# A decoder layer in one kernel: load order of a weight pair, sums of squares folded ahead of TensorE, one of the last multiplications moved to GpSimd

## The chip, the cores and the metric

The kernel runs on one core of one Trainium2 chip. The time is the device time of one execution in microseconds (us), and the median of the runs stands for a kernel. One execution is taken with the hardware profiler; its trace gives the start and length of every instruction. The engines are called PE (TensorE), DVE (VectorE), ACT (ScalarE), POOL (GpSimd) and SP (SyncE, which issues the DMA transfers here).

## The reference

`x` is 1024 tokens by 1024 features, `mem` 256 tokens by 1024, all in float32, one layer:

```python
h = rmsnorm(x, ln1); z = h @ w_in                      # x and mem: sums of squares over the features
x = x + concat(mlstm(z), forgetting_attention(z)) @ w_out
x = x + cross_attention(rmsnorm(x, ln_x), rmsnorm(mem, ln_mem), w_xq, w_xkv, w_xo)
u = relu(rmsnorm(x, ln2) @ w_ff1)                      # up projection, 1024 -> 4096
x = x + (u * u) @ w_ff2                                # down projection
return rmsnorm(x, ln_f)
```

`rmsnorm(x, g)` is `x * rsqrt(mean(x*x) + eps) * g` for each token. The mLSTM part has gates of each token (log-sigmoid, cumulative sums) and a short causal convolution ahead of it.

## The kernel before

Features lie on the 128 partitions and tokens along the free axis. Every float32 product is done as three matmuls in a reduced format: `split` cuts an operand into a high part (ACT, L134) and the rest (DVE, L135), and `mm3` issues the matmuls of lines L186 to L188. Weight tiles of 128x1024 are loaded to `wr` or `z` and cut into `wh` and `wl`.

**Order.** A scheduler with a simulated timeline decides, when the program is built, in which order the instructions of each engine stand, except inside `in_order()` blocks, which keep the written order (the start of the kernel, and the last part). On the chip each engine works through its queue strictly in that order. PSUM banks go by names (`mm`, `tp`, `m2`, `sc`, `ov`), and a new tile of a name waits until an old one of it has been read out.

**Stages.** First come the values and gates of the mLSTM, with the sums of squares of `x` (two halves of 512 tokens) and of `mem`; then projections, the heads of the mLSTM, forgetting attention, cross attention, the up projection, the down projection, and the last part with the final norm.

**Sums of squares.** ACT squares pairs of feature tiles into the 128x1024 tiles `wide`, and DVE adds these up (`add_to`, L370), so that the two feature tiles of a pair stand side by side: element `[p, e*512 + t]`. `rsqrt_sums` sums over the partitions with matmuls against a column of ones (L234). It needs two matmuls for each 128 tokens, one for each `e`. For one half of `x` that is 8 matmuls, for `mem` 4, and `rsqrt_cols` makes the inverse roots `rcol` of them on DVE and POOL.

**Gates.** The gate values get their log-sigmoid by a polynomial on DVE (L440), then PE transposes them (`mm`, `sc`: L456; `tp`, `sc`: L461), and DVE runs two scans (L462, L466) along the tokens.

**Up projection.** Each pair of weight tiles `r1`, `r2` (128x1024, four blocks x11, x12, x21, x22 of 512) feeds seven products instead of eight. `raw_pair` (L1235) loads both tiles, `left_up` cuts blocks and has POOL form the sums of blocks: first `x21 + x22`, both in `r2` (L1256), then three differences (L1223) and a last addition (L1260). The products of the pairs follow one another with weights prepared five products ahead. POOL also folds parts of the results (L1223, `r_f`).

**The end.** The tokens of the last half are done in two quarters of 256. `finish` sums the squares (L1603), makes the inverse roots, spreads them over the partitions into a PSUM bank (`spread`, L213), and DVE multiplies four tiles of 128x2x256 by them (L1617), each followed by its store on SP's queue (L1618).

Of the kernel before, what the change touches and what calls it, by code (L numbers as in the profile page):

```python
# [11 lines left out]
AF = mybir.ActivationFunctionType  # L12
ALU = mybir.AluOpType
# [4 lines left out]
P = 128  # L18
T = 1024
TH = 512  # L20
D = 1024
KT = D // P
NM = 256
# [21 lines left out]
def hybrid_layer(ctx: ExitStack, tc: tile.TileContext, a: dict, out: bass.AP):  # L45
    nc = tc.nc
    v, s, g = nc.vector, nc.scalar, nc.gpsimd
# [31 lines left out]
    def w2(tag, n=512, dt=F32, p=P):  # L79
        return sb("r_" + tag, [P, 512], BUFS[tag], dt)[:p, :n]  # L80
# [15 lines left out]
    def ov_():  # L96
        return ps_tile("ov")
# [16 lines left out]
    ones = const("ones", [P, 1])  # L114
# [79 lines left out]
    def rsqrt_cols(out_, sums, scale, n, over=None):  # L194

        var = col("var", n)
        if over is None:
            v.tensor_scalar(out=var, in0=sums, scalar1=scale, scalar2=EPS, op0=ALU.mult, op1=ALU.add)
        else:
            e = col("t", n)  # L200
            v.scalar_tensor_tensor(out=e, in0=over, scalar=EPS, in1=over, op0=ALU.mult, op1=ALU.mult)
            v.scalar_tensor_tensor(out=var, in0=sums, scalar=scale, in1=e, op0=ALU.mult, op1=ALU.add)
        y = col("y", n)
        g.tensor_tensor(out=y, in0=var, in1=half[:, :n], op=ALU.pow)
        t = col("t", n)
        v.tensor_tensor(out=t, in0=y, in1=y, op=ALU.mult)
        v.scalar_tensor_tensor(out=t, in0=t, scalar=-0.5, in1=var, op0=ALU.mult, op1=ALU.mult)
        v.scalar_tensor_tensor(out=out_, in0=t, scalar=1.5, in1=y, op0=ALU.add, op1=ALU.mult)

    def spread(ps, cols, n):  # L210

        for t in range(n):
            nc.tensor.matmul(ps[:, t * P : (t + 1) * P], cols[:, t : t + 1].broadcast_to([P, P]), ident, start=True, stop=True)  # L213

    def sum_cols(ps, src, n):
        for t in range(n):
            nc.tensor.matmul(ps[:, t : t + 1], src[:, t * P : (t + 1) * P], ones, start=True, stop=True)

    def square_sum(acc, x, first, by=s, add=v):
        sq = acc if first else w2("c")[:, : x.shape[-1]]  # L220
        if by is s:
            s.activation(sq, x, AF.Square)
        else:
            by.tensor_tensor(out=sq, in0=x, in1=x, op=ALU.mult)
        if not first:
            add.tensor_tensor(out=acc, in0=sq, in1=acc, op=ALU.add)

    def rsqrt_sums(acc, r, nt, parts=1, bank=None, over=None):

        ps = (bank or ov_)()  # L230
        for t in range(nt):
            for e in range(parts):
                at = (e * nt + t) * P
                nc.tensor.matmul(ps[:, t : t + 1], acc[:, at : at + P], ones, start=e == 0, stop=e == parts - 1)  # L234
        rsqrt_cols(r, ps[:, :nt], 1.0 / D, nt, over)

    def rsqrt_row(acc, r, nt, parts=1, bank=None, over=None):

        rsqrt_sums(acc, r, nt, parts, bank, over)
        rb = (bank or ov_)()  # L240
        spread(rb, r, nt)
        return rb[:, : nt * P]

    rowd = dram.tile([4, T], F32, name="rowd")

# [10 lines left out]
    rcol = const("rcol", [P, 8])  # L256
# [11 lines left out]
    at = 0  # L268
# [10 lines left out]
    rcol_m = const("rcol_m", [P, 2])  # L279

    def mem_prepare():
        acc = w2("b")
        for i in range(KT // 2):
            raw = w2("ffde"[i])
            load(raw.rearrange("p (k c) -> p k c", k=2), a["mem"][:, 2 * i : 2 * i + 2])
            traced = len(nc.cur_bb.bb.instructions)
            square_sum(acc, raw, i == 0)
            hi = w2("p", dt=F32R)
            for e in range(2):
                c = slice(e * NM, e * NM + NM)  # L290
                gain = vec[:, VEC["ln_mem"] + 2 * i + e :][:, 0:1]
                split(hi[:, c], raw[:, c].bitcast(F32R), raw[:, c], gain)
            for x in nc.cur_bb.bb.instructions[traced:]:
                if i > 1 and x.engine == mybir.EngineType.Activation:
                    tc.add_manual_dep(
                        x,
                        last_evicted.name,
                        mybir.DependencyInfo(mybir.DependencyClass.NoSync, mybir.DependencyReason.DATA),
                        reason="behind the first values",
                    )  # L300
            for p_, t in enumerate((hi.bitcast(F32), raw)):
                load(hmd[:, p_, 2 * i : 2 * i + 2], t.rearrange("p (k c) -> p k c", k=2))
        rsqrt_sums(acc, rcol_m, 2, 2)


    xa = act(F32)
# [21 lines left out]
    raws = [sb("wr", [P, 1024], 2) for _ in range(2)]  # L328
    wg_raw = z4()[:, : KT * 16].rearrange("p (k c) -> p k c", k=KT)
    for k in range(KT):  # L330
        if k == 1:
            load(wg_raw, a["w_gate"])
        if k % 2 == 0:
            c = slice(k % 4 * 256, k % 4 * 256 + 512)
# [28 lines left out]
    wide = [w4() for _ in range(3)]  # L363
# [5 lines left out]
    def add_to(t, u):  # L369
        return v.tensor_tensor(out=t, in0=t, in1=u, op=ALU.add)  # L370
# [3 lines left out]
    z, e, q, lf = (small[:, i:j].rearrange("p (t c) -> p t c", c=c) for i, j, c in ((0, 128, GC), (128, 224, GW), (224, 320, GW), (320, 416, GW)))  # L374
# [6 lines left out]
    with in_order():  # L381
        for k in range(KT):
            cut_w(k)
            cut_x(0, k)
            if k in (0, 2, 4):
                cut_gates(k // 2)
            if k in (1, 3, 5):
                square_to(wide[k // 2], 0, k)
            if k == 4:
                add_to(wide[0], wide[1])  # L390
            first_values(0, k, range(4))
        square_to(wide[1], 0, 7)
        cut_x(1, 0)
        add_to(wide[0], wide[2])
        cut_x(1, 1)
        add_to(wide[0], wide[1])
        for k in range(2, 6):
            cut_x(1, k)
        for k in range(KT):
            if k in (2, 3):  # L400
                cut_x(1, k + 4)
            if k == 2:
                square_to(wide[1], 1, 1)
            if k == 4:
                square_to(wide[2], 1, 3)
            first_values(1, k, range(3))
            if k == 1:
                rsqrt_sums(wide[0], rcol[:, 0:4], 4, 2)
            if 2 < k < 7:
                first_sink(0, k - 3)  # L410
            if k == 6:
                add_to(wide[1], wide[2])
                square_to(wide[0], 1, 5)
        square_to(wide[2], 1, 7)
        add_to(wide[1], wide[0])
        last_sum = add_to(wide[1], wide[2])
    tiles[1].append(ps_tile("mm")[:, :WV])
    for k in range(KT):
        first_values(1, k, (3,))
    rsqrt_sums(wide[1], rcol[:, 4:8], 4, 2)  # L420
    for t in range(4):
        first_sink(1, t)
    last_evicted = next(i for i in reversed(nc.cur_bb.bb.instructions) if i.engine == mybir.EngineType.Activation)
# [5 lines left out]
    ps = ov_()  # L429
# [263 lines left out]
    for _ in range(2):  # L693
        t = act().rearrange("p a b -> p (a b)").rearrange("p (i c) -> p i c", i=4)
# [404 lines left out]
    n = 0  # L1099
# [36 lines left out]
    for n0 in (0, 4):  # L1136
        ws = [weights(a["w_out_b"][n0 // 2 + i], 6 * P) for i in range(2)]
        for hf in range(2):
            if len(h2) <= hf:
                h2.append((act(), act()))  # L1140
            for n in range(n0, n0 + 4):
                w = both(ws[n // 2 % 2], lambda t: t.rearrange("p (k c) -> p k c", k=3)[:, :, n % 2 * P : n % 2 * P + P])
                ps = mm()
# [87 lines left out]

    def raw_pair(p_, n0, n1):
        raws = [sb("wr", [P, 1024], 2) if p_ % 2 else z4()[:, :1024] for _ in range(2)]
        for raw, n in zip(raws, (n0, n1)):
            load(raw, a["w_ff1"][n])  # L1235
        return raws

    todo = [(b, k, 4 * b + k, 4 * b + 2 + k) for b in range(NB) for k in range(2)]

# [354 lines left out]
    def finish(acc, hf, c0, wid, parts):  # L1594

        n = wid // P
        r, var, e, y_, t = (col(c, n) for c in ("r", "var", "den", "y", "t"))
        over = inv[:, 4 * hf + c0 // P :][:, :n]
        v.scalar_tensor_tensor(out=e, in0=over, scalar=EPS, in1=over, op0=ALU.mult, op1=ALU.mult)
        ps = bank()  # L1600
        for i in range(n):
            for k in range(parts):
                nc.tensor.matmul(ps[:, i : i + 1], acc[:, k * wid + i * P :][:, :P], ones, start=k == 0, stop=k == parts - 1)  # L1603
        v.scalar_tensor_tensor(out=var, in0=ps[:, :n], scalar=1.0 / D, in1=e, op0=ALU.mult, op1=ALU.add)
        g.tensor_tensor(out=y_, in0=var, in1=half[:, :n], op=ALU.pow)
        yield
        v.tensor_tensor(out=t, in0=y_, in1=y_, op=ALU.mult)
        v.scalar_tensor_tensor(out=t, in0=t, scalar=-0.5, in1=var, op0=ALU.mult, op1=ALU.mult)
        v.scalar_tensor_tensor(out=r, in0=t, scalar=1.5, in1=y_, op0=ALU.add, op1=ALU.mult)
        yield  # L1610
        rb = bank()[:, :wid]
        spread(rb, r, n)
        rb = rb.rearrange("p (o c) -> p o c", o=1).broadcast_to([P, 2, wid])
        yield
        for k in range(0, KT, 2):
            y = x2[k // 4][:, k // 2 % 2, :, hf, c0 : c0 + wid]
            v.tensor_tensor(out=y, in0=y, in1=rb, op=ALU.mult)  # L1617
            load(out[:, k : k + 2, hf * TH + c0 : hf * TH + c0 + wid], y)  # L1618
            yield

# [82 lines left out]
```

## Time and profile before

| | before |
|---|---|
| median of 3 runs | 1522.53 us (1522.43 to 1523.9) |
| the profiled execution | 1523.35 us |
| its span in the trace | 1521.6 us |
| granted TensorE clock | 0.998 |
| busy: PE / DVE / ACT / POOL | 1502.7 / 1100.3 / 727.7 / 510.1 us |
| matmuls on PE | 7694 |

The span runs from the first to the last instruction that the trace shows; 1.75 us of the profiled execution lie around it. Times in the trace count from the span's start. A row of the timeline has the start, the length, the engine, the line, the operation, what is written and read, and, in brackets, how long the engine sat idle ahead of it and what ended that. A PE row's length overlaps the next; consecutive 128x512 matmuls start 0.23 us apart.

### The profile page before, as it was taken

Reading aid. Unit: us, or ns where it says so; the run is one execution under the profiler, and the core shown is the slowest. Engines: PE = TensorE matmul, PEld = TensorE weight load, DVE = VectorE, ACT = ScalarE, POOL = GpSimd, SP = SyncE. Lnnn points to the kernel's source line nnn. Section 1 sums busy time; section 2 is a strip of 40 time slices with the busy share of each in tenths; the row PEclk is TensorE's granted clock in tenths of the full one; section 3 lists DMA queues with packets and bytes.
Section 4 is the critical chain, followed back from the end, with each engine's and each line's share of the span. In section 5 each row is a group of like instructions: output and inputs, shape, how many; then the busy total and the mean of one; then the engine's idle time right before and its main releaser. Section 6 shows DMA issues by size and latency. Waiting matters only on the chain.

```text
span 1521.6 us, 21977 instructions
## 1 busy us (share of the span) xinstructions
PE 1502.7 (99%) x7694; PEld 1261.5 (83%) x7694; DVE 1100.3 (72%) x1743; ACT 727.7 (48%) x1360; POOL 510.1 (34%) x543
## 2 busy tenths in 40 slices
PE   9999999999999999999999999999999999999997
PEld 9988888889999788888888877778787888888887
DVE  7766676765787786944457989898887667787665
ACT  7324343334687665644443456666664621122124
POOL 1003030413364442511110034544555265663322
PEclk9999999999999999999999999999999999999999
DMA  6322223435888886843344437776678777776623
GB/s 239 109 77 87 98 100 114 135 126 157 246 244 267 260 264 230 300 131 124 119 147 157 153 134 277 247 256 242 222 252 286 291 277 276 276 270 248 239 94 111
DMA packets 122538, 299.86 MB, mean 197 GB/s; under 512 B 13614, under 2 KB 28264, under 8 KB 115516
## 3 DMA queue, kind: packets, MB, share of 16 engines
q1 hardware_dynamic: 122428, 298.46, 57.4%
q8 instruction: 60, 0.98, 0.3%
q14 instruction: 50, 0.41, 0.1%
HBM read 199.60 MB, written 98.81 MB: 196 GB/s over the span
## 4 chain that ended last, share of the span: by engine, by line
PE 93%; DVE 3%; ACT 2%; DMA 1%; issue 1%; SPq 0%; DVEq 0%; POOLq 0%; POOL 0%; ACTq 0%
PE tp L186 8%; PE tp L187 8%; PE tp L188 8%; PE m L186 6%; PE sc L186 6%; PE m L187 6%; PE m L188 6%; PE sc L187 6%; PE sc L188 6%; PE mm L186 6%; PE mm L187 6%; PE mm L188 6%; PE ov L186 2%; PE ov L187 2%; PE ov L188 2%; PE ov L801 2%
## 5 line engine op out<-in xcount | busy, mean ns | idle before, releaser
L186 PE MATMUL tp<-act,wl 128*128 128x512 f32 (+1 forms) x440 | 172.9, 393 | 1.2 <-ACT row L1396 0.7
L187 PE MATMUL tp<-act,wh 128*128 128x512 f32 (+1 forms) x440 | 172.1, 391 | 0.0
L188 PE MATMUL tp<-act,wh 128*128 128x512 f32 (+1 forms) x440 | 171.7, 391 | 0.0
L135 DVE TENSOR_TENSOR wl<-wr,wh 128x1024 fp32r<-128x1024 f32 (+2 forms) x95 | 124.5, 1311 | 22.0 <-ACT wh L134 21.4
L134 ACT ACTIVATE wh<-wr 128x1024 fp32r<-128x1024 f32 (+2 forms) x95 | 95.6, 1007 | 75.9 <-PE tp L188 34.7
L186 PE MATMUL mm<-act,wl 128*128 128x512 f32 (+1 forms) x332 | 127.5, 384 | 0.0
L188 PE MATMUL mm<-act,wh 128*128 128x512 f32 (+1 forms) x332 | 127.3, 383 | 0.0
L187 PE MATMUL mm<-act,wh 128*128 128x512 f32 (+1 forms) x332 | 127.2, 383 | 0.0
L186 PE MATMUL m<-act,wl 128*128 128x512 f32 (+1 forms) x308 | 117.7, 382 | 0.5 <-DVE wl L135 0.5
L188 PE MATMUL m<-act,wh 128*128 128x512 f32 (+1 forms) x308 | 117.7, 382 | 0.0
L187 PE MATMUL m<-act,wh 128*128 128x512 f32 (+1 forms) x308 | 117.5, 381 | 0.0
L186 PEld LDWEIGHTS tp<-act,wl 128*128 128x128 f32 x440 | 82.6, 188 | 20.6 <-ACT row L1396 1.2
L188 PEld LDWEIGHTS tp<-act,wh 128*128 128x128 f32 x440 | 82.6, 188 | 18.9
L187 PEld LDWEIGHTS tp<-act,wh 128*128 128x128 f32 x440 | 82.7, 188 | 18.5
L186 PE MATMUL sc<-act,wl 128*128 128x512 f32 (+1 forms) x248 | 97.0, 391 | 1.0 <-DVE wl L135 1.0
L188 PE MATMUL sc<-act,wh 128*128 128x512 f32 (+1 forms) x248 | 96.7, 390 | 0.0
L187 PE MATMUL sc<-act,wh 128*128 128x512 f32 (+1 forms) x248 | 96.6, 390 | 0.0
L1467 POOL TENSOR_TENSOR z<-wr 128x256 f32<-128x256 f32 x56 | 51.7, 944 | 130.6 <-DMA wr<-w_ff2q 116.8
L134 ACT ACTIVATE wh<-z 128x1024 fp32r<-128x1024 f32 (+1 forms) x54 | 55.5, 1028 | 80.8 <-POOL z L1467 58.4
L135 DVE TENSOR_TENSOR wl<-z,wh 128x1024 fp32r<-128x1024 f32 (+1 forms) x54 | 74.3, 1376 | 7.8 <-ACT wh L134 7.6
L134 ACT ACTIVATE w<-wr 128x768 fp32r<-128x768 f32 (+2 forms) x31 | 25.5, 823 | 106.2 <-PE tp L186 33.7
L188 PEld LDWEIGHTS mm<-act,wh 128*128 128x128 f32 x332 | 62.3, 188 | 12.7
(726 smaller groups left out, 4288.4 us busy)
## 6 DMA issues: line engine op xcount, KB each, us to landing
act<-right SPq DMA_DIRECT2D x49, 1024.0 KB
right<-w SPq DMA_DIRECT2D x56, 256.0 KB
wr<-w_ff2q SPq DMA_DIRECT2D x28, 512.0 KB
right<-r_d SPq DMA_DIRECT2D x49, 256.0 KB
right<-r_e SPq DMA_DIRECT2D x49, 256.0 KB
act<-fqk SPq DMA_DIRECT2D x48, 256.0 KB
wr<-w_in SPq DMA_DIRECT2D x20, 512.0 KB
wr<-w_ff SPq DMA_DIRECT2D x20, 512.0 KB
```

What stands on the lines that cost most here:

```text
L134: s.activation(hi, src, AF.Copy)
L135: return v.tensor_tensor(out=lo, in0=src, in1=hi.bitcast(F32), op=ALU.subtract)
L186: nc.tensor.matmul(ps, w[1], x[0], start=first, stop=False, skip_group_check=more)
L187: nc.tensor.matmul(ps, w[0], x[1], start=False, stop=False, skip_group_check=more)
L188: nc.tensor.matmul(ps, w[0], x[0], start=False, stop=last, skip_group_check=more)
L801: nc.tensor.matmul(self.ov[:, c0:], self.fv[:, self.j], t[:, c0:], start=self.j == 0 and t is self.p[1], stop=self.last and t is self.p[0])
L1467: g.tensor_tensor(out=o, in0=x, in1=y, op=op)
```

## The change

There are three edits, and the scheduler's answer to them.

1. `raw_pair` issues the load of the second tile of a pair, `r2`, ahead of that of `r1`. The places of the loads in SP's queue stay.
2. A new helper `fold` adds the second half of a tile of sums to its first half on DVE. It stands behind the last `add_to` of each half of `x` (128x512) and behind the squares of `mem` (128x256). The sums over the partitions then take half the matmuls, through `sum_cols` (L217): 4, 4 and 2 in place of 8, 8 and 4.
3. In `finish`, for the last quarter alone, the second multiplication is done otherwise: ACT copies the spread roots from PSUM to `r_c` (L1615), and POOL multiplies the 128x2x256 tile by them (L1616). Its store stays the second of the last four in the program's text.

```diff
+    def fold(x, n):
+        return v.tensor_tensor(out=x[:, :n], in0=x[:, :n], in1=x[:, n : 2 * n], op=ALU.add)
...
-    def rsqrt_sums(acc, r, nt, parts=1, bank=None, over=None):
-        ps = (bank or ov_)()
-        for t in range(nt):
-            for e in range(parts):
-                at = (e * nt + t) * P
-                nc.tensor.matmul(ps[:, t : t + 1], acc[:, at : at + P], ones, start=e == 0, stop=e == parts - 1)
-        rsqrt_cols(r, ps[:, :nt], 1.0 / D, nt, over)
+    def rsqrt_sums(acc, r, nt):
+        ps = ov_()
+        sum_cols(ps, acc, nt)
+        rsqrt_cols(r, ps[:, :nt], 1.0 / D, nt)
...
-        rsqrt_sums(acc, rcol_m, 2, 2)
+        fold(acc, NM)
+        rsqrt_sums(acc, rcol_m, 2)
...
         add_to(wide[0], wide[1])
+        fold(wide[0], TH)
...
-                rsqrt_sums(wide[0], rcol[:, 0:4], 4, 2)
+                rsqrt_sums(wide[0], rcol[:, 0:4], 4)
...
-        last_sum = add_to(wide[1], wide[2])
+        add_to(wide[1], wide[2])
+        last_sum = fold(wide[1], TH)
...
-    rsqrt_sums(wide[1], rcol[:, 4:8], 4, 2)
+    rsqrt_sums(wide[1], rcol[:, 4:8], 4)
...
-        for raw, n in zip(raws, (n0, n1)):
+        for raw, n in zip(raws, (n1, n0)):
             load(raw, a["w_ff1"][n])
-        return raws
+        return raws[::-1]
...
+            if k == 2 and hf and c0:
+                rs = w2("c", wid)
+                s.activation(rs, rb, AF.Copy)
+                g.tensor_tensor(out=y, in0=y, in1=wide_(rs), op=ALU.mult)
+            else:
+                v.tensor_tensor(out=y, in0=y, in1=wide_(rb), op=ALU.mult)
```

Since the scheduler is run again, the queues change beyond the edited lines: PE's order in the start (behind the first values) and around the end of cross attention, with that of DVE and ACT there, and POOL's in the up projection. The helpers' lines move by 3 to 7, so L456, L461 and L477 of before are L452, L457 and L473 now, L1396 is L1392, L1372 is L1368, L1256 is L1252, and L1223 is L1219.

PE, behind the projections that follow the first values. `tp` in the first row and `sc`, `mm` are projections of 128x256; L456 and L461 are the transposes of the gates; the `tp` and `m` with 128x512 use the next two weight tiles. Before:

```order
L188 MATMUL tp_678<-wh_505,act_104 128x256
L456 MATMUL mm_622<-ident,w_29_148 12x128 x4
L456 MATMUL sc_628<-ident,w_29_148 12x128 x4
L461 MATMUL sc_634<-ident,w_29_148 4x128 x4
L186 MATMUL sc_705<-wh_499,act_105 128x256
...
L477 MATMUL ov_759<-ident,act_486 128x4 x8
L186 MATMUL tp_887<-act_104,wl_856 128x512
...
L186 MATMUL m_95_928<-act_102,wl_925 128x512
```

The same place in the changed kernel:

```order
L188 MATMUL tp_672<-wh_499,act_105 128x256
...
L186 MATMUL tp_880<-act_104,wl_849 128x512
...
L452 MATMUL mm_616<-ident,w_29_148 12x128 x4
L452 MATMUL sc_622<-ident,w_29_148 12x128 x4
L457 MATMUL sc_628<-ident,w_29_148 4x128 x4
L186 MATMUL sc_699<-wh_493,act_105 128x256
...
L473 MATMUL ov_753<-ident,act_480 128x4 x8
L186 MATMUL m_95_921<-act_102,wl_918 128x512
```

The 24 matmuls of the 128x512 `tp` stood between the transposes' followers (L477) and `m`; now they stand ahead of the transposes, right behind the `tp` of 128x256, and `m` follows L473 directly. On DVE the split that makes the weights of `m` stands behind both scans, before and now; of the changed kernel:

```order
L458 SCALAR_TENSOR_TENSOR act_480<-w_41_481,act_480 12x1024
L461 TENSOR_TENSOR act_480<-sc_628,act_480 4x512
L461 TENSOR_TENSOR act_480<-tp_633,act_480 4x512
L138 SCALAR_TENSOR_TENSOR w_64_774<-act_480,w_63_773 12x1024
L462 SCALAR_TENSOR_TENSOR act_480<-act_480 4x1024
L138 SCALAR_TENSOR_TENSOR act_107<-sc_699,rcol,act_107 128x2x128
L135 TENSOR_TENSOR wl_918<-wr_915,wh_917 128x1024
```

Here L458 and L462 are the two scans; they wait for the transposes, and `wl_918` is what `m_95_921` reads. Nothing in this row of seven moved against another.

PE around the end of cross attention, where `tp` and `sc` are the banks of one output tile each, filled in two passes (`act_8402`, then `act_8601`), and the second pass of a bank waits until ACT has read the first. Before:

```order
L188 MATMUL sc_9143<-act_8402,wh_9063 128x512
L186 MATMUL tp_9125<-act_8601,wl_8790 128x512
...
L186 MATMUL m_1717_9202<-act_8728,wl_9118 128x512
...
L186 MATMUL ov_9246<-act_8729,wl_9118 128x512
...
L186 MATMUL sc_9143<-act_8601,wl_9064 128x512
```

The same place in the changed kernel:

```order
L188 MATMUL mm_9069<-act_7775,wh_9048 128x512
L186 MATMUL tp_9118<-act_8594,wl_8783 128x512
...
L186 MATMUL sc_9136<-act_8395,wl_9057 128x512
...
L188 MATMUL tp_9118<-act_8594,wh_8782 128x512
...
L186 MATMUL sc_9136<-act_8594,wl_9057 128x512
...
L186 MATMUL m_1717_9195<-act_8721,wl_9111 128x512
```

Before, 12 matmuls of `m` and 9 of `ov` stood between the second pass of `tp` and that of `sc`; now the second pass of `sc` follows the last four matmuls of `tp` directly, and `m` comes behind it. The second pass of `tp`, in turn, now has 24 matmuls of `mm` between itself and the first. ACT's queue holds, now as before, the cut of a weight tile, the read of `tp` and the read of `sc` in this order there.

POOL in the up projection, one window of it; L1256 (now L1252) is `x21 + x22` of a pair, and `r_f` is a fold of a result. Before:

```order
L1260 TENSOR_TENSOR wr_9435<-wr_9435,r_c_9444 128x512
L1223 TENSOR_TENSOR r_f_9515<-w_1749_9470,r_f_9515 128x512
L1256 TENSOR_TENSOR wr_9776<-wr_9776 128x512
L1223 TENSOR_TENSOR z_1767_9606<-z_1767_9606,z_1766_9605 128x512
```

The same window in the changed kernel:

```order
L1256 TENSOR_TENSOR wr_9429<-wr_9429,r_c_9437 128x512
L1252 TENSOR_TENSOR wr_9768<-wr_9768 128x512
L1219 TENSOR_TENSOR r_f_9508<-w_1749_9463,r_f_9508 128x512
L1219 TENSOR_TENSOR z_1766_9598<-z_1766_9598,z_1767_9599 128x512
```

The addition now stands ahead of the fold `r_f` in two of every three windows; in the third it stays behind it. In all of them it waits for the first load of its pair, where it waited for the second.

At the end, DVE's four multiplications of the last quarter become three, and ACT and POOL get one instruction each; SP's last four stores stand in another order, the second and third of them exchanged.

More of the change, by code (lines that the diff above doesn't have):

```diff
@@ L226, in square_sum @@
             add.tensor_tensor(out=acc, in0=sq, in1=acc, op=ALU.add)
-    def rsqrt_sums(acc, r, nt, parts=1, bank=None, over=None):
-        ps = (bank or ov_)()
-        for t in range(nt):
-            for e in range(parts):
-                at = (e * nt + t) * P
-                nc.tensor.matmul(ps[:, t : t + 1], acc[:, at : at + P], ones, start=e == 0, stop=e == parts - 1)
-        rsqrt_cols(r, ps[:, :nt], 1.0 / D, nt, over)
[L237 to L242, printed above, removed]
+    def rsqrt_sums(acc, r, nt):
+        ps = ov_()
+        sum_cols(ps, acc, nt)
+        rsqrt_cols(r, ps[:, :nt], 1.0 / D, nt)
     rowd = dram.tile([4, T], F32, name="rowd")
@@ L1612, in finish @@
         spread(rb, r, n)
-        rb = rb.rearrange("p (o c) -> p o c", o=1).broadcast_to([P, 2, wid])
+        wide_ = lambda x: x.rearrange("p (o c) -> p o c", o=1).broadcast_to([P, 2, wid])
         yield
@@ L1616, in finish @@
             y = x2[k // 4][:, k // 2 % 2, :, hf, c0 : c0 + wid]
-            v.tensor_tensor(out=y, in0=y, in1=rb, op=ALU.mult)
+            if k == 2 and hf and c0:
[4 more added lines that the diff above has]
+                v.tensor_tensor(out=y, in0=y, in1=wide_(rb), op=ALU.mult)
             load(out[:, k : k + 2, hf * TH + c0 : hf * TH + c0 + wid], y)
```

## The prediction

> **What bounds the kernel now.** I read the page first, then PE's waits, then the chain of waits in the three regions that the change touches, and the timelines of the engines there.
>
> ```profile
> span 1521.6 us, 21977 instructions
> ...
> PE 1502.7 (99%) x7694; PEld 1261.5 (83%) x7694; DVE 1100.3 (72%) x1743; ACT 727.7 (48%) x1360; POOL 510.1 (34%) x543
> ```
>
> PE is busy for 1502.7 of 1521.6 us. So a microsecond is gained only where PE has fewer matmuls to issue, where one of its few waits goes, or behind its last matmul; one is lost wherever a new wait opens in PE's queue. PE's waits name what there is to win:
>
> ```profile
> PE mm L213 <- DVE c_r L1609: 1.6, 1, 1.6
> ...
> PE sc L186 <- DVE wl L135: 1.0, 2, 0.5
> ...
> PE tp L186 <- DVE wl L135: 0.5, 1, 0.5
> PE m L186 <- DVE wl L135: 0.5, 1, 0.5
> ```
>
> The columns are total, times and longest. Four waits of 0.5 us for a weight split (`wl`) lie in the up projection. The wait for `c_r` belongs to the final norm and stays.
>
> **Part one, the folds.** The chain shows what the sums cost on PE:
>
> ```profile
> 23.08 1.68 PE ov L234 x16
> ...
> 39.71 1.68 PE ov L234 x16
> ...
> 74.40 0.79 PE ov L234 x8
> ```
>
> Each written matmul shows as two records. Half of them go: 0.84 + 0.84 + 0.39 = 2.07 us less on PE. DVE gets three additions for it. The same operation at the fold's size, and the last addition ahead of the first fold, are these:
>
> ```profile
> 20.86 1.22 DVE L370 TENSOR_TENSOR w<-w,w 128x1024 f32<-128x1024 f32 x1
> ...
> 45.96 0.68 DVE L226 TENSOR_TENSOR r_b<-r_c,r_b 128x512 f32<-128x512 f32 x1
> ```
>
> The addition ends at 22.08, the fold at about 22.7, and PE comes to the sums at 23.08: 0.3 us to spare, so the first fold is hidden, as the cuts behind it on DVE are needed later still. The other two stand where PE has other matmuls queued ahead of the sums. I take the folds at nothing and the gain at **-2.07**. If the 0.3 us were gone, the price is at most the fold's 0.68.
>
> **What the scheduler moved in the start.** The 24 matmuls of 128x512 `tp` now follow the 128x256 `tp` directly, and the gates' transposes come behind them. Two waits follow. PE's rows of before, from the chain (first the transposes' end and the moved group, then `m`) and the timeline:
>
> ```profile
> 54.28 0.60 PE L456 MATMUL mm<-ident,w 128*12 128x128 f32 x4
> ```
>
> ```profile
> 61.41 0.58 PE ov L477 x8
> 61.99 0.43 PE tp L186
> ...
> 67.78 0.24 PE m L186
> ```
>
> What ACT and DVE do for them:
>
> ```profile
> 54.43 0.47 ACT L137 ACTIVATE act<-tp,rcol 128x256 fp32r<-128x256 f32 x1 [2.35 <-PE tp L188]
> ```
>
> ```profile
> 54.94 0.48 DVE L138 SCALAR_TENSOR_TENSOR act<-tp,rcol,act 128x256 fp32r<-128x256 f32 x1 [0.71 <-ACT act L137]
> 56.02 2.28 DVE L462 TENSOR_TENSOR_SCAN act<-w,act 12x1024 f32<-12x1024 f32 x1 [0.60 <-ACT act L457]
> ...
> 60.74 2.27 DVE L466 TENSOR_TENSOR_SCAN act<-act 4x1024 f32<-4x1024 f32 x1
> ...
> 63.31 1.20 DVE L135 TENSOR_TENSOR wl<-wr,wh 128x1024 fp32r<-128x1024 f32 x1
> ```
>
> First wait: the moved group takes the bank of the 128x256 `tp`, so it starts only when ACT and DVE have read that. Before, PE was free at 54.28 and the second read ended at 55.42 (54.94 + 0.48): about **+1.2** with the signal. Second wait: the weights of `m` are cut behind two scans, and the scans need the transposes. From the first transpose to the end of the cut: 63.31 + 1.20 - 54.28 = 10.2 us. Between transpose and `m` PE had work until 67.78, which covered it by 3.3 us; without the moved group's 5.8 us (61.99 to 67.78) the work ends 7.7 us after the transpose, and PE waits 10.2 - 7.7 = 2.5, with the restart **+2.6**. Both are waits that the trace of before doesn't show. From below their bound is nothing (if the scheduler's picture holds on the chip), from above 1.2 and 2.6; I take the upper end, since the chain is made of rows of this same place.
>
> **The end of cross attention.** ACT and PE of before:
>
> ```profile
> 876.27 0.50 PE L186 MATMUL tp<-act,wl 128*128 128x512 f32 x1 [0.73 <-ACT row L1396]
> ...
> 879.18 0.39 PE L186 MATMUL m<-act,wl 128*128 128x512 f32 x1
> ...
> 884.08 0.39 PE L186 MATMUL sc<-act,wl 128*128 128x512 f32 x1
> ```
>
> ```profile
> 879.38 1.06 ACT L134 ACTIVATE wh<-wr 128x1024 fp32r<-128x1024 f32 x1 [2.11 <-PE tp L188]
> 880.34 0.58 ACT L1372 ACTIVATE r_p<-tp 128x512 f32<-128x512 f32 x1
> 880.82 0.59 ACT L1396 ACTIVATE row<-sc 128x512 f32<-128x512 f32 x1
> ```
>
> The wait at 876.27 (0.73 idle; 0.9 with the restart, as 0.50 idle makes 0.66 in the up projection below) goes, because 24 other matmuls now stand in between. But `sc`, which came at 884.08, now follows the second pass of `tp`, whose end was 879.18. It needs the read that ended at 881.41, behind a cut and a read that themselves wait for that pass. That makes a wait of 881.41 - 879.18 = 2.2, with the restart 2.35; net **+1.45**. Its lower bound is -0.9, if ACT gets to the read earlier.
>
> **Part two, the load order.** DVE, POOL and PE in one of the four windows with a wait for `wl`, and DVE at the same work in the next window:
>
> ```profile
> 1015.44 0.69 DVE L1383 TENSOR_TENSOR r_p<-sc,r_p 128x512 f32<-128x512 f32 x1 [1.18 <-PE sc L188]
> ...
> 1017.85 2.39 DVE L135 TENSOR_TENSOR w<-w,r_e 128x512 fp32r<-128x512 f32 x2
> ...
> 1036.12 1.29 DVE L135 TENSOR_TENSOR w<-w,r_d 128x512 fp32r<-128x512 f32 x2
> ```
>
> ```profile
> 1018.37 1.31 POOL L1256 TENSOR_TENSOR wr<-wr 128x512 f32<-128x512 f32 x1 [5.79 <-DMA wr<-w_ff]
> 1019.65 1.75 POOL L1223 TENSOR_TENSOR z<-z,z 128x512 f32<-128x512 f32 x1
> ```
>
> ```profile
> 1023.64 0.40 PE L188 MATMUL tp<-act,wh 128*128 128x512 f32 x1
> 1024.54 0.50 PE L186 MATMUL m<-act,wl 128*128 128x512 f32 x1 [0.50 <-DVE wl L135]
> ```
>
> ```profile
> 1009.21 0.33 SPq L1235 DMA_DIRECT2D wr<-w_ff  x1
> ...
> 1013.69 0.33 SPq L1235 DMA_DIRECT2D wr<-w_ff  x1
> ```
>
> POOL had waited 5.79 us for the second load of a pair, which took 4.68 us from its issue (1013.69 to 1018.37); when it came, the addition ran beside DVE's splits, and two of those took 2.39 us instead of 1.29: DVE lost 1.1 us, and PE's next start came 0.90 after the last, 0.66 more than the usual 0.24. With `r2` loaded first, the addition's data is there as long after 1009.21, at 1013.9, and it runs where DVE has 1.18 us idle (to 1015.44). DVE's 1.1 us come back, more than the 0.66 that PE waits. Four such windows: **-2.65**. The bound on the other side is nothing, if the waits stay. What could be late next is the cut of `r1`, now loaded second: but the pair loaded here is `wr`, while the window still works on the pair in `z`, so the cut has the rest of the window; I take nothing for it.
>
> [...]
>
> **Part three, the end.**
>
> ```profile
> 1515.56 2.48 DVE L1617 TENSOR_TENSOR act<-act,mm 128x512 f32<-128x512 f32 x4 [1.18 <-PE mm L213]
> ```
>
> ```profile
> 1511.51 0.42 ACT L1635 ACTIVATE r_b<-act 128x256 f32<-128x256 f32 x1 [0.39 <-DVE act L1633]
> ```
>
> ```profile
> L1542 POOL TENSOR_TENSOR act<-act 128x512 f32<-128x512 f32 x8 | 11.3, 1417 | 18.0 <-DVE act L1572 17.8
> ```
>
> Four multiplications of 0.62 us end at 1518.04, and the last store follows. Now ACT's copy (0.42, near 0.5 with the signals) reads the bank that DVE reads, so I put it behind DVE's first multiplication: 1515.56 + 0.62 + 0.5 = 1516.7. POOL needs 1.42 for this size: 1518.1. The third store waits for it, and the fourth stands behind the third on SP: about 0.5 later than before. Bounds: nothing, if copy and multiplication run side by side, and 1.0, if POOL takes the 1.75 of the window above: **+0.5**.
>
> **The sum:** -2.07 + 1.2 + 2.6 + 1.45 - 2.65 + 0.5 = +1.0 us. The profiled execution took 1523.35 (1521.6 in the span, 1.75 around it), so 1524.4 for that; it lay 0.8 above the median of 1522.53, so **1523.5** as a median. 0.2% is 3.05 us, about what a measurement of this kernel can tell from no change; the forecast lies within it.
>
> **The rivals.**
>
> *The new waits are covered (faster).* The three waits of the start and of cross attention are read from an order, with times of a kernel that didn't have them. If ACT and DVE come to those reads earlier, because their queues were reordered too, they vanish, and the wait at 876.27 still goes: -2.07 - 0.9 - 2.65 + 0.5 = -5.1, so 1517.4. For it: the scheduler chose that order by a timeline of its own. Against: `wl` stands behind both scans in DVE's queue, and 10.2 us of rows can't shrink to 7.7. Chance 0.25.
>
> *The addition meets DVE elsewhere (slower).* In two of three windows POOL's addition now stands ahead of `r_f` and runs at a new time. Where it lands on DVE's cut of a group:
>
> ```profile
> 1033.02 1.23 DVE L135 TENSOR_TENSOR wl<-z,wh 128x1024 fp32r<-128x1024 f32 x1 [0.33 <-ACT wh L134]
> ...
> 1038.60 0.69 DVE L1383 TENSOR_TENSOR r_p<-sc,r_p 128x512 f32<-128x512 f32 x1 [0.59 <-PE sc L188]
> ```
>
> DVE has 0.33 + 0.59 = 0.92 us idle around it. It decides when the loss passes 0.92: at 1.1 DVE is 0.2 late, at POOL's whole 1.31, 0.4. DVE then carries its lateness into the next window, and the four waits stay (2.65 not won) while four others of about 0.4 open: +1.0 + 2.65 + 1.6 = +5.2, so 1527.8; with the old waits alone, 1526.2. Against: DVE is idle in each window. Chance 0.31. [...]
>
> *Nothing changes.* The sums' matmuls could stand where PE waits anyway, as the first values' evictions follow them, and the additions in the up projection could keep their time, if the loads were bound by transfers and not by their order: 1522.5. PE's waits list none behind the sums. Chance 0.06.
>
> **How the numbers follow.** My forecast has 0.38; with the third rival, 0.44 lie within 0.2%. Faster is 0.25, slower 0.31. The range reaches from the first rival, 1517.4, to a little above the second, 1528.0; the forecast's own is 1521.8 (no first wait, nothing at the end) to 1524.7 (a fold that shows, 1.0 at the end).
>
> **What would show it.** The sums as x8, x8 and x4 records of half the time; a wait of about 1.2 us ahead of the 128x512 `tp` near 54 us and one of 2.6 us ahead of `m` near 69 us, named after DVE's `wl`; 2.3 us ahead of `sc` near 880 us; no wait for `wl` in the up projection; the last store issued half a microsecond later, counted from the spread. I am wrong if PE goes through the start without those waits, or if waits for `wl` remain in the up projection.

## The result, and the profile after

The changed kernel is slower by 0.35%: 1527.99 us at the median of 8 runs (1524.45 to 1530.41), before 1522.62 (8 runs), ratio 1.0035 with a 95% interval of 1.0024 to 1.0045. The profiled execution took 1530.41 us. The page and PE's waits of it:

```profile
span 1528.7 us, 21939 instructions
...
PE 1504.1 (98%) x7674; PEld 1262.2 (83%) x7674; DVE 1100.2 (72%) x1745; ACT 728.6 (48%) x1361; POOL 507.0 (33%) x544
```

```profile
PE m L186 <- DVE wl L135: 2.6, 1, 2.6
PE sc L186 <- ACT row L1392: 2.1, 1, 2.1
...
PE mm L213 <- DVE c_r L1605: 1.6, 1, 1.6
...
PE tp L186 <- DVE act L138: 1.1, 1, 1.1
...
PE tp L536 <- DVE r_e L135: 1.0, 1, 1.0
PE sc L186 <- DVE act L138: 0.5, 1, 0.5
```

The four waits for `wl` in the up projection are gone, and others stand in their place: ahead of `m` (2.6), of `sc` (2.1), of the 128x512 `tp` (1.1), of the products L536 of a head's keys and values (1.0) and of a product of the first values near 29 us (the last row, 0.5). PE shows 20 records fewer, which are 10 written matmuls, and still its busy time grew by 1.4 us. PE's timeline shows the waits, and why the busy time grew (start, length; in brackets the idle time ahead and what ended it):

```profile
53.21 0.28 PE L188 MATMUL tp<-wh,act 128*128 128x256 f32 x1
54.58 0.50 PE L186 MATMUL tp<-act,wl 128*128 128x512 f32 x1 [1.08 <-DVE act L138]
```

```profile
885.08 0.40 PE L188 MATMUL tp<-act,wh 128*128 128x512 f32 x1
887.59 0.71 PE L186 MATMUL sc<-act,wl 128*128 128x512 f32 x1 [2.12 <-ACT row L1392]
888.10 0.63 PE L187 MATMUL sc<-act,wh 128*128 128x512 f32 x1
888.53 0.63 PE L188 MATMUL sc<-act,wh 128*128 128x512 f32 x1
```

Behind the wait near 885 us the matmuls start 0.43 us apart instead of 0.23. The same stands behind the wait ahead of `m`. The view by windows gives the busy times of the engines and, before the DMA share, the granted clock:

```profile
72.00:75.00 3.00, 3.00 (x8) 2.34 (x8) 2.90 (x4) 0.00 (x0) 0.00 (x0) 0.50 0.51 171
...
78.00:82.00 4.00, 4.00 (x22) 3.30 (x21) 1.38 (x2) 0.83 (x2) 0.00 (x0) 1.00 0.67 245
```

PE's granted clock fell to 0.50 behind each of the two waits (72 to 75 us, the first row, and 889 to 891 us), for about eight matmuls. From the first matmul to the first that starts at the full rate again, 14 intervals took 4.91 us behind the wait ahead of `m` and 9 took 3.76 behind the other; at 0.23 us each, with 0.34 for the first, they would have taken 3.37 and 2.21. So each of these waits of over 2 us cost about 1.5 us more than the wait itself, 3.1 together.

The sums of the second half of `x`, from the chain, and the window of the up projection that answers to the one shown of before (POOL, then DVE):

```profile
41.59 0.79 PE ov L217 x8
```

```profile
1023.18 1.36 POOL L1252 TENSOR_TENSOR wr<-wr 128x512 f32<-128x512 f32 x1 [1.49 <-DMA wr<-w_ff]
1027.17 1.68 POOL L1219 TENSOR_TENSOR z<-z,z 128x512 f32<-128x512 f32 x1 [2.64 <-DVE r_c L135]
```

```profile
1024.60 0.69 DVE L1379 TENSOR_TENSOR r_p<-sc,r_p 128x512 f32<-128x512 f32 x1 [1.23 <-PE sc L188]
...
1027.01 2.39 DVE L135 TENSOR_TENSOR w<-w,r_e 128x512 fp32r<-128x512 f32 x2
1029.32 0.68 DVE L1219 TENSOR_TENSOR w<-w,r_p 128x512 f32<-128x512 f32 x1
```

In the window of before, DVE's operation behind the splits was this one:

```profile
1020.16 1.79 DVE L1223 TENSOR_TENSOR w<-w,r_p 128x512 f32<-128x512 f32 x1
```

The addition now runs in DVE's idle time, as forecast. The splits still take 2.39 us, with POOL's next operation beside them; the operation behind them is the one that is quick again, 0.68 us where it took 1.79. So DVE's 1.1 us came back, but not in the rows from which the prediction took them. In the window of before, POOL's addition ended at 1019.68, DVE's splits at 1020.24, POOL's next operation at 1021.40, DVE's next at 1021.95: both of these DVE rows overlap rows of POOL. Which engine held up the other there, and for how long, no run tests.

The end:

```profile
1522.21 0.69 DVE L1618 TENSOR_TENSOR act<-act,mm 128x512 f32<-128x512 f32 x1 [0.87 <-PE mm L213]
1523.41 1.29 DVE L1618 TENSOR_TENSOR act<-act,mm 128x512 f32<-128x512 f32 x2 [0.51 <-ACT r_c L1615]
```

```profile
1522.99 0.38 ACT L1615 ACTIVATE r_c<-mm 128x256 f32<-128x256 f32 x1 [3.56 <-DVE act L1618]
```

```profile
1523.45 1.27 POOL L1616 TENSOR_TENSOR act<-act,r_c 128x512 f32<-128x512 f32 x1 [2.70 <-ACT r_c L1615]
```

ACT's copy waits for DVE's first multiplication, and DVE's second for the copy. From the first multiplication to the end of the span it takes 6.49 us, before 6.04. The other profiles agree: 6.45 to 6.53 us in the four others with the GpSimd multiplication, 6.03 to 6.11 in six others without it.

### The profile page after: what moved, and what is told of

Its sections match the earlier page's. It is cut to its first block, busy times and chain, and to the rows that moved or that the text cites. A ratio compares the mean times of both kernels' runs of the same rounds, so it can differ in the third digit from the quotient of the medians.

```text
span 1528.7 us, 21939 instructions
## 1 busy us (share of the span) xinstructions
PE 1504.1 (98%) x7674; PEld 1262.2 (83%) x7674; DVE 1100.2 (72%) x1745; ACT 728.6 (48%) x1361; POOL 507.0 (33%) x544
## 4 chain that ended last, share of the span: by engine, by line
PE 89%; DMA 5%; DVE 2%; ACT 1%; issue 1%; POOL 0%; SPq 0%; POOLq 0%; DVEq 0%; ACTq 0%
PE tp L186 8%; PE tp L188 8%; PE tp L187 8%; PE sc L186 6%; PE sc L187 6%; PE sc L188 6%; PE m L188 6%; PE m L186 6%; PE m L187 6%; PE mm L186 5%; PE mm L188 5%; PE mm L187 5%; PE ov L186 2%; PE ov L187 2%; PE ov L188 2%; PE ov L797 2%
## 5 line engine op out<-in xcount | busy, mean ns | idle before, releaser
L135 DVE TENSOR_TENSOR wl<-z,wh 128x1024 fp32r<-128x1024 f32 (+1 forms) x54 | 77.4, 1433 | 10.3 <-ACT wh L134 10.3
```

The lines of the kernel that those rows point to most:

```text
L135: return v.tensor_tensor(out=lo, in0=src, in1=hi.bitcast(F32), op=ALU.subtract)
```

## The experiments

The account by waits says that the loss comes from the reordered start, which the folds bring, and from the second pass of `sc`, which the load order brings. Its rivals put it on the folds' work itself, on POOL's addition in the up projection, or on the end.

**The folds alone.**

```diff
 (kernel before)
+fold(...) behind each half's last add_to and behind the squares of mem; rsqrt_sums with half the matmuls
```

> The kernel before with the folds alone; load order and the end as before. The account by waits: the reordered start comes with the folds. On PE the sums are 2.07 us shorter; against that stand the waits that the changed kernel's profile shows: about 0.65 ahead of a product at 28 us, 1.24 ahead of the 128x512 tp, 2.7 ahead of m, 1.2 ahead of the L536 transposes near 102 us, and 1.4 us of matmuls at half rate behind the wait of 2.7. Sum +5.1, so about 1527.7 us against 1522.6, or +3.7 in executions in which the rate doesn't fall. The rival account, by which the loss comes from the load order and from the end: the folds alone gain 1 to 2 us, so about 1521.

Measured: 1527.25 us, ratio 1.0035 (1.0022 to 1.0047). PE's waits in its profile:

```profile
PE m L186 <- DVE wl L135: 3.1, 2, 2.6
...
PE tp L186 <- DVE act L138: 1.1, 1, 1.1
PE tp L536 <- DVE r_e L135: 1.0, 1, 1.0
```

The waits of the start are there one for one, and the ratio is that of the changed kernel: the folds, with the order that they bring, carry the loss as far as these runs can tell.

**The load order alone.**

```diff
-        for raw, n in zip(raws, (n0, n1)):
+        for raw, n in zip(raws, (n1, n0)):
...
-        return raws
+        return raws[::-1]
```

> The kernel before with the load order of a pair alone. The account by waits: the four waits for wl in the up projection go (-2.65) and the wait of 0.9 at 875 us too, a new one of 2.3 opens ahead of the second pass of sc there, followed by 1.85 us of matmuls at half rate. Sum +0.6, so about 1523.2 us; -1.25 where the rate doesn't fall. The rival of the prediction, by which POOL's addition meets DVE elsewhere: waits for wl remain in the up projection, +2 to +5 us. By the prediction's first rival: -3.5.

Measured: 1522.11 us, ratio 0.9995 (0.9986 to 1.0004), no difference that these runs resolve. Its profile:

```profile
PE sc L186 <- ACT row L1396: 2.1, 1, 2.1
...
PE tp L186 <- DVE r_f L1383: 0.4, 1, 0.4
```

The wait of 2.1 comes with the load order. No slow matmul followed it in this execution. The waits for `wl` are gone; one of 0.4 for `r_f` came, far from what the second rival of the prediction needs.

**The multiplication on GpSimd alone.**

```diff
+            if k == 2 and hf and c0:
+                s.activation(rs, rb, AF.Copy)
+                g.tensor_tensor(out=y, in0=y, in1=wide_(rs), op=ALU.mult)
```

> The kernel before with the multiplication on GpSimd alone. By the prediction +0.5 us (0 to 1.0), so 1523.1; the profile of the changed kernel shows from PE's last start to the end of the span hardly a difference, so that a value near +0.0 is as likely. A rival by which the end carries the loss: +3 or more.

Measured: 1522.84 us against 1522.8, ratio 1.0004 (0.9995 to 1.0013). The end carries none of the loss that can be seen at the median; the 0.45 us of the traces are less than these runs resolve.

**The changed kernel with PE's old order in the start.**

```diff
+            if hf and "gcol" in marks:      # in conv_silu: first matmul of the 128x512 tp
+                keep_behind(marks.pop("gcol"), start)   # an order, no wait: behind the first L473 transposes
```

> The changed kernel, all its parts, with one added order: the 128x512 tp is kept behind the first L473 transposes, where it stood before. The account by waits: the waits of 1.24 and 2.7, the half rate behind the latter (1.4) and the wait of 1.2 near 102 us go, so 6.5 us less than the changed kernel, about 1521.5 us, with the wait at 28 us left. The rival by which the folds' work on DVE is itself what costs: no change, about 1528.

Measured: 1523.53 us, ratio 1.0005 (0.9996 to 1.0013): 4.5 us less than the changed kernel, so the order did cost; but 2 us more than expected. Its waits, its DVE near 54 us, and the same place of before:

```profile
PE mm L452 <- DVE w L437: 2.4, 1, 2.4
```

```profile
53.80 0.48 DVE L138 SCALAR_TENSOR_TENSOR act<-tp,rcol,act 128x256 fp32r<-128x256 f32 x1 [1.00 <-ACT act L137]
54.20 1.12 DVE L436 SCALAR_TENSOR_TENSOR w<-w 128x96 f32<-128x96 f32 x4
55.36 0.26 DVE L437 SCALAR_TENSOR_TENSOR w<-w 128x96 f32<-128x96 f32 x1
```

```profile
53.97 0.26 DVE L441 SCALAR_TENSOR_TENSOR w<-w 128x96 f32<-128x96 f32 x1
```

The gates' polynomial ends on DVE (its last step is L441, now L437), and PE's transposes wait for it. Before, it ended at 54.23 and PE began at 54.28: no wait, but no slack either. Now PE is there about 1.1 us earlier, mostly since its sums are shorter, and the polynomial ends 1.4 us later, at 55.62: the roots come 0.75 us later (their last step, L208, starts at 43.86 instead of 43.11), the fold of `mem`'s squares (0.41 us) stands ahead of it on DVE, and a read of `tp` that waits 1.00 us for ACT stands among its steps. In the changed kernel the 128x512 `tp` stands in this hole.

**The gates kept early as well.** The load order, the folds, no GpSimd multiplication, the start's order as in the run above, and:

```diff
+        if c == 1 and t == 5:   # in mv_sink: DVE's read of the 128x256 tp, an order behind the last gate step
+            tc.add_manual_dep(x.ins, last_gate.ins.name, ...)
...
+    jobs.insert(3, jobs.pop(4))   # second pass of sc behind the 12 matmuls of m, by an order of the same kind
```

> The load order with the second pass of sc kept behind m, as in the run beside it; the folds, with the 128x512 tp kept behind the first L473 transposes and, on DVE, the read of the 128x256 tp kept behind the last step of the gates' polynomial; no multiplication on GpSimd. Theory: the gates' polynomial on DVE sets when PE's transposes can start; the folds and the moved read made it end 1.4 us later than before, while PE came 1.1 us earlier. Kept in order, it should end near 54.2 us, the wait of 2.58 shrink to about 1.0, and the folds be worth -2.07 + 0.65 + 1.0 = -0.4 against the run beside it: about 1519.4. The rival, by which PE's shorter sums are worth their 2.07 once the order is mended: about 1517.7. If the folds cost by themselves: 1521 or more.

Measured: 1523.11 us, ratio 1.0007 (0.9999 to 1.0016).

```profile
PE m L186 <- DVE r_f L1397: 1.4, 1, 1.4
...
PE tp L186 <- DVE r_f L1397: 1.2, 2, 0.9
PE mm L454 <- DVE w L439: 1.1, 1, 1.1
PE m L186 <- DVE wl L135: 0.9, 1, 0.9
PE sc L186 <- DVE r_f L1397: 0.9, 1, 0.9
```

```profile
54.90 0.60 PE L454 MATMUL mm<-ident,w 128*12 128x128 f32 x4 [1.07 <-DVE w L439]
```

The wait for the gates shrank from 2.4 to 1.1, as the theory has it, but the transposes still start at 54.90, before at 54.28: up to there the folds of `x` gain nothing even so. The total missed by 3.7 us, because waits for `r_f` of 3.5 us together stand in the up projection here. What brought them in this kernel and not in the others with the same load order wasn't settled.

**The load order with distance for the second pass.**

```diff
 (kernel before, load order as above)
+    jobs.insert(3, jobs.pop(4))
...
+            tc.add_manual_dep(new[0], five, ...)   # product (1, 2) behind product (0, 5)
```

> The kernel before with the load order, and one added order on PE: the second pass of sc at the end of cross attention is kept behind the 12 matmuls of m (the fifth product of the first pair). If the wait of 2.28 us there is what eats the gain of the load order, 12 x 0.235 = 2.8 us of m cover it: about -2.65 - 0.9 + 0.7 (what the load order alone still showed of waits in the up projection) = -2.9 us against before, near 1519.8. The rival, by which the second pass only moves the wait to the next user of ACT's reads: no change against the load order alone, about -0.7.

Measured: 1521.01 us, ratio 0.9997 (0.9988 to 1.0006).

```profile
PE m L186 <- DVE wl L135: 1.9, 1, 1.9
```

That is the rival's case, no change against the load order alone: the wait moved to `m`, whose weights weren't cut yet.

**Made waits of six lengths.**

```diff
+    def pause(at, ps, ended):     # kernel before; ahead of the first product of 24 steps of the down projection
+        s.activation(scratch[:, 0:TH], ended, AF.Copy)
+        for n in LENGTHS[(at + at // 6) % 6]:
+            s.activation(scratch[:, :n], scratch[:, :n], AF.Copy)
+        nc.tensor.matmul(ps[:, :1], scratch[:, :P], ones, start=True, stop=True)
```

> The kernel before with 24 made waits of PE in the down projection, one ahead of each step's first product in six of its seven blocks: a 128x1 matmul waits for 1 to 4 copies on ACT that start when the step before has ended, which makes waits of about 0.85, 1.35, 1.8, 2.3, 2.75 and 3.7 us, four of each, with 42 matmuls of 128x512 between two of them. If PE's granted clock falls when it has been idle long enough, matmuls at a start-to-start of 0.43 us follow the long waits, in some cases of 2.3 and 2.75 us and in most of 3.7, and none the short ones. The rival, by which the slow matmuls near 72 and 888 us came from their place (transfers or weights of that moment): none here after any wait. Together the waits are 4 x 12.8 = 51 us, so about 1574 us without slow matmuls, and 1.4 to 2 us more for each wait that is followed by them.

Measured: 1655.49 us in the one execution taken, where 1574 and up to 2 us for each slow event were expected. The waits were longer than planned, 74.7 us together instead of 51, since ACT had a weight cut of its own ahead of the copies; slow matmuls make about 35 us, and over 20 of the 133 us above the kernel before stay unexplained. So only the rows are used here, not the total. Three of the waits, and the clock behind each:

```profile
1230.87 0.38 PE L1552 MATMUL m<-ones,row 128*128 128x1 f32 x2 [1.18 <-ACT row L1549]
...
1340.67 0.38 PE L1552 MATMUL sc<-ones,row 128*128 128x1 f32 x2 [2.78 <-ACT row L1551]
...
1403.67 0.38 PE L1552 MATMUL sc<-ones,row 128*128 128x1 f32 x2 [1.69 <-ACT row L1549]
```

```profile
1229.00:1236.00 7.00, 5.83 (x26) 4.44 (x26) 4.65 (x5) 2.34 (x4) 2.32 (x2) 1.00 1.02 430
...
1403.60:1408.00 4.40, 4.33 (x13) 3.46 (x14) 1.48 (x2) 0.02 (x1) 2.20 (x3) 0.62 0.43 164
...
1342.00:1346.00 4.00, 4.00 (x19) 3.23 (x18) 1.37 (x2) 0.00 (x0) 4.00 (x5) 1.00 0.30 48
```

| idle time ahead of the matmul | waits | followed by slow matmuls | how many slow ones |
|---|---|---|---|
| 1.18 us | 1 | 0 | |
| 1.69 to 2.29 us | 5 | 5 | 7 or 8 |
| 2.75 to 2.80 us | 4 | 3 | 6 to 8 |
| 3.23 to 3.46 us | 5 | 4 | 11 to 13 |
| 3.87 us and more | 8 | 8 | 7 to 13 |

The 24th matmul of this kind shows no wait and no slow matmul. Slow means 0.43 us from start to start, so each costs 0.19 us, and an event about 1.2 to 2.5 us. Slow matmuls follow at 20 places all along the down projection, far from the two of the changed kernel, so the transfers or weights of one moment are not the cause. Idle time brings them, and not each time: a wait of 2.78 and one of 3.44 us had none behind them. Between 1.18 us, of which there is one, and 1.69 us nothing was measured.

**The wait filled**, with the changed kernel again as its control:

```diff
+                for i in range(6):   # ahead of m's own matmuls, in its bank
+                    nc.tensor.matmul(ps, ident, h[0][0][:, i].bitcast(F32), start=True, stop=True)
```

> The changed kernel with six matmuls of 128x512 in the bank of the 128x512 m ahead of its own, kept behind the first L473 transposes; they compute nothing that is kept, and fill the wait of 2.7 us there with work. PE comes to m no sooner, so by the account of waits without the clock: no change against the changed kernel in the same call. By the account with the clock, its matmuls behind the wait run at full rate in each execution, where they lost 1.4 us in the profiled ones: about 1 to 1.4 us less at the median, and no matmul at a start-to-start of 0.43 us near 72 us in the profile. The slow ones behind the wait near 885 us stay possible.

> The changed kernel once more, as the control of the run beside it and for a second profile: about 1528 us, 1.0035 of before. The waits of 1.2, 2.7, 1.2 and 2.3 us at the same places, since they follow from the order; the matmuls at half rate behind those of 2.7 and 2.3 us in part, since in the other runs they followed three of six such waits; executions with the granted clock at 0.998 near 1524.5, those at 0.995 near 1529.

Measured: 1528.05 us filled and 1527.42 the control (1.0036 both); the gain of 1 to 1.4 us that was expected did not come. The filling was mis-sized: as float32 its six matmuls took 4.8 us, not 2.7. So the median tells nothing of the clock. Windows of the filled kernel, then of the control:

```profile
70.00:72.00 2.00, 2.00 (x6) 0.92 (x5) 2.00 (x4) 0.04 (x1) 0.00 (x0) 1.00 0.34 59
72.00:74.00 2.00, 2.00 (x8) 1.22 (x7) 2.00 (x4) 0.00 (x0) 0.00 (x0) 1.00 0.61 215
```

```profile
70.00:74.00 4.00, 3.59 (x9) 2.84 (x10) 4.00 (x6) 0.18 (x2) 0.00 (x0) 0.59 0.47 135
104.50:108.00 3.50, 3.50 (x12) 2.85 (x12) 1.15 (x4) 1.29 (x4) 0.29 (x1) 0.55 0.21 75
887.00:891.00 4.00, 3.25 (x14) 2.66 (x15) 4.00 (x6) 2.53 (x6) 0.83 (x1) 1.00 0.62 197
```

With PE kept busy the clock stayed at 1.00 in this one execution, where it fell in all three profiles that have the wait of 2.6 (the changed kernel twice, 0.50 from 72 to 75 us and 0.59 from 70 to 74 us, and the folds alone, whose mean over the span is 0.996 where before has 0.998). In the control it also fell near 105 us, to 0.55, behind the wait ahead of L536, but not behind the wait of 2.1 near 887 us (1.00), where it had in the first (0.59 in the same window). The same program thus has the same waits, while the clock falls behind one in some executions and not in others: that of 2.1 stands in five profiles, and slow matmuls follow it in two. What the clock costs at the median is not shown.

**What can be kept.** DVE makes the sums of the first two pairs and POOL those of the others. The load order from the third pair on leaves PE's order at the end of cross attention as it was:

```diff
+        late = p_ > 1
-        for raw, n in zip(raws, (n0, n1)):
+        for raw, n in zip(raws, (n1, n0) if late else (n0, n1)):
...
-        return raws
+        return raws[::-1] if late else raws
```

> The kernel before with the load order of a pair from the third pair on, where POOL makes the sums; the first two pairs, whose sums DVE makes, are loaded as before. PE's order at the end of cross attention is then that of before, with its wait of 0.9 us near 875 us and none of 2.28, so no matmul at half rate there. Up projection as in the load order alone: the four waits of 0.66 go, 0 to 0.7 us of others come. About -2.65 to -2.0 against before, near 1520. If the first two pairs' order carried the gain, or if the waits in the up projection come back in other windows: about 1522.5.

Measured: 1519.81 us, ratio 0.9974 (0.9962 to 0.9986). At the end of cross attention stands the wait of before, and none for `wl` or `r_f` in the up projection:

```profile
PE tp L186 <- ACT row L1397: 0.7, 1, 0.7
```

The same with the fold of `mem` alone:

```diff
+        v.tensor_tensor(out=acc[:, :NM], in0=acc[:, :NM], in1=acc[:, NM:], op=ALU.add)
-        rsqrt_sums(acc, rcol_m, 2, 2)
+        rsqrt_sums(acc, rcol_m, 2)
```

> The run beside it with the fold of mem's squares alone (128x256 on DVE, four matmuls down to two); nothing of the gates hangs on it, and PE's order stays. If a fold is worth its matmuls where no chain on DVE sets the pace: 0.39 us less than the run beside it, which is less than these runs resolve; its profile should show two matmuls with 128x1 near 74 us and no new wait near them. If a fold costs wherever it stands: waits of DVE near 74 us, and a time above the run beside it.

```profile
74.68 0.34 PE ov L234 x4
```

Measured: 1519.24 us, ratio 0.9970 (0.9959 to 0.9982). The sums are shorter by half, and no wait stands near them; whether 0.4 us were gained, these runs can't tell. Against what was expected, something of the gates does hang on this fold: it stands ahead of their polynomial on DVE, and PE's transposes near 54 us now wait 0.2 us for the last step. Both versions are faster than the kernel before; the changed kernel, measured apart from them, was slower than it.

## Why the prediction was right, and where its sum failed

The prediction had a small loss as the likeliest, 1523.5 us, with 0.38, and a range to 1528.0. The measured 1527.99 lies 0.01 us inside that range and above the forecast's own range, which ended at 1524.7. The range reached so far only for the second rival's sake, and that rival did not occur: that the number falls inside is luck. What was right is the sign and the three waits. Point by point:

- **The waits read from the new order** were right in place, size and releaser: 1.08 idle ahead of `tp` (1.2 forecast), 2.6 ahead of `m` (2.6), 2.1 ahead of `sc` (2.35 with the restart). The first rival, that they are covered, falls.
- **The load order's -2.65** was right: the four waits are gone, though DVE gets its 1.1 us back one operation later than forecast.
- **The end's +0.5** came out as 6.49 - 6.04 = +0.45 in the span, on the mechanism described; the median can't show it.
- **The folds "at nothing"** is the step of the sum that failed. The first fold wasn't hidden: the roots came 1 us later, since DVE was 0.6 us later with the sums' result and POOL's operation for the roots then took 2.09 us instead of 1.01, with a cut on DVE beside it from its start (25.69 and 25.70 us), where before the cut began 0.55 us later than POOL. A further cut stands behind the roots in DVE's queue, and PE waited 0.5 us, 0.65 with the restart, ahead of the product near 29 us that needs it. That is the 0.68 which the prediction named as the most. What it did not see at all is the DVE chain that follows the sums: the trace of before has the polynomial's end at 54.23 us and PE's transposes at 54.28, so with PE's old order the shorter sums only end in a wait (2.4 us, or 1.1 with the gates kept early). With the order that the folds bring, the moved `tp` and the waits of 1.1 and 2.6, which the sum has, stand there instead. The folds alone, with all that they bring, cost 4.5 us.
- **Not in the sum at all** were the clock and the wait ahead of L536. In the profiled execution they are 3.1 us of slow matmuls and 1.0 us idle, with the restart 1.2; the clock is the largest term that is missing there. The wait comes from PE's new order as well: L536 needs the transposes of the keys (L523) by way of DVE, ACT and DVE, 2.7 us from 100.26 to 102.97, and 5 matmuls of `mm` now stand in between where 24 stood before; the prediction didn't walk through this part of the order. Together with the 0.65 near 29 us that makes +1.0 + 0.65 + 1.2 + 3.1 = about +6.0, where the span grew by 7.1. About 1.1 us arose between 350 and 600 us, where PE's order is that of before and the kernels tried differ by as much (the folds alone come out 0.85 us shorter there); 0.7 of it is a longer wait for a transfer (`z` from `mix`, 1.0 instead of 0.3), which in the other profiles lies anywhere up to 1.6; what moves it isn't shown.
- **The second rival**, the addition meeting DVE elsewhere, gave 1527.8 us and so the right number for a wrong reason: the changed kernel has no wait for `wl` or `r_f` in the up projection. Its four waits of 0.4 assume that DVE loses POOL's whole 1.31 us; no run shows such a loss: the rows of before give 1.1.

The clock explains the spread of the 8 executions in part only. At 1528 us, 0.001 of mean granted clock is 1.5 us. The one execution with 0.998 took 1524.45 us; the other seven had 0.994 to 0.997 and took 1526.4 to 1530.4, but the three at 0.996 alone lie between 1526.9 and 1530.4. That the fastest lies close to the 1524.4 that was forecast for a profiled execution doesn't confirm the sum either: without the slow matmuls the profiled execution would still have taken about 1527.3.

## What to carry to other kernels

Work taken off the busiest engine can be worth nothing ahead of a point where it already meets another engine's chain without slack, as the folds' was here, even if no wait is listed there: look at who ends just before it. When a scheduler reorders a queue, walk through the new order with the old durations; the three waits looked for here came out to about a tenth of a microsecond, but two that weren't looked for, of 0.5 and 1.0 us, were missed, so the walk has to cover every place where a queue changed. A rewrite that helps one stage can be confined to the part of the loop where it helps, so that the order elsewhere stays.

## What the runs showed of the hardware that I had not expected

In the run of made waits, matmuls that started 0.43 us apart, 6 to 13 of them, followed 20 of the 22 idle times of 1.69 us and more, and not the one of 1.18 us. The granted clock over the windows shown of that run was 0.62 behind 1.69 us idle, and 1.00 behind 1.18 and behind one of 2.78, where no slow matmul followed. In one profile of the changed kernel it fell to 0.50 behind 2.58 us idle and behind 2.12. In the other it was 0.59 behind the first of these waits, 1.00 behind the second, and 0.55 from 104.5 to 108 us, behind 1.0 us idle that was followed by 1.86 us of short matmuls (103.03 to 104.89 us in the first profile, which has 1.00 behind them).
